# Value products of both key tiles in one step, and whole-width transposes for the gate columns, in a hybrid streaming encoder layer

## The chip, the cores and the metric

The kernel runs on one core of one Trainium2 chip. The metric is the device time of one execution in microseconds (us), lower is better. The kernel before took 2306.43 us as the median of three runs, with 2305.89 and 2309.27 at the ends. A core has a matrix engine (TensorE, "PE" in the profile; its weight loads are listed apart as "PEld"), a vector engine (VectorE, "DVE"), an engine for activation functions and copies (ScalarE, "ACT"), a general engine (GpSimd, "POOL"), a queue that issues most transfers (SyncE, "SP"), and sixteen DMA engines. TensorE reads its operands from the on-chip buffer and writes its results into banks of an accumulation memory (PSUM), from where ScalarE or VectorE copies them out.

## The reference

The kernel computes one layer of an encoder for a prompt of 2048 tokens and, beside it, eight short decode sequences of 16 tokens. Everything is float32. Cut to what matters here:

```
qm, km, vm, om, ip, fp, qa, ka, va = split_in(x @ w_in)
hm = mlstm_chunkwise(qm, km, vm, logi, logf, ...)      # 4 heads x 128, a matrix memory per head
ha = swa_prompt(rope(qa), rope(ka), va, attn_sinks)    # 8 query heads on 2 key/value heads x 64
h = layer_norm(ALPHA * x + concat(gated hm, ha) @ w_out)
y = layer_norm(ALPHA * h + conv_ffn(h))
```

The part that the change touches first is the attention over a sliding window. A query tile of 128 tokens sees its own tile and the one before, under a mask:

```
s = einsum(q, k) * 64 ** -0.5                 # per head, masked
mx = maximum(max(s), sink)
p = exp(s - mx) / (sum(exp(s - mx)) + exp(sink - mx))
o = einsum(p, v)                              # the value products
```

The second part is the matrix memory. There the weight of key s for token l is `exp(b_l - b_s + logi_s - m_l)`, with `b` the running sum of the logarithms of the forget gate and `m` a running maximum. The kernel holds these exponents as rows (one head per partition, tokens along the row) and also needs them as columns (one token per partition), since ScalarE adds a bias per partition.

## The kernel before, in words

The work has four stages on TensorE: the input projections (up to about 640 us), the output projection (to about 903 us), the up-projections of the feed-forward part (to about 1860 us) and its down-projections. The large products are done by a seven-product scheme on halves, each number split into two parts of fewer bits and multiplied in three products (lines 705, 731, 223 to 225, 1874 and 2081).

The mLSTM and the attention are woven into the first two stages. Two chains of small steps, `m_chain` (line 1044) and `a_chain` (line 1246), each a Python generator, run through the sixteen prompt tiles. A planner, `Chains` (line 158), walks over the dense products. Each dense step (six products of 256 columns, or three of 512) adds 645 to its clock. A chain's step yields its cost, which is added to the clock, the delay after which its next step is due, and how many of the five small PSUM banks the next step needs. Each request for a bank notes the time at which it is reckoned to be free: the clock plus `HOLDS`, or 3500 where the bank's name isn't in it (`bank`, line 928). A step is put into the stream as soon as the clock has passed its due time and the banks it needs are reckoned free. TensorE's order is exactly this order (`manual_schedule`, line 237); the other engines' orders are worked out by the framework from the dependences. The waits on the chip are real semaphores, so a step that the planner puts too early makes TensorE wait, and the dense products behind it wait as well.

One attention tile (`swa`, line 1272) does these steps: the scores of four heads (line 1304, tile `psc`), the exponentials and the scores of the other four, the divisions by the sums (line 1321), and then the part that the change edits. The probabilities lie with queries on partitions, in `sc`; for the value products the keys must lie on partitions. So, for each key tile, eight 128 x 128 transposes (line 1343, tile `ppt`) and two copies by ScalarE (line 1344, tile `pth`) turn them. The value products (line 1349, tile `ppo`) take the 64 columns of a head's values as the stationary operand and the 512 columns of four query heads as the moving one, one product for each half of the output's partitions. Each such product is two instructions in the profile. The step before runs the transposes of a key tile together with the value products of the key tile before:

```
for kt in range(nk + 1):
    ... transposes of key tile kt, if kt < nk ...
    ... value products of key tile kt - 1, if kt ...
```

After the first transposes the queries and keys of the next tile are turned as well (`swa_first`, line 1259, tiles `pq` and `pk`). A last copy by ScalarE (line 1356, tile `mixa`) and a store end the tile.

The mLSTM's tile (`m_tile`, line 1183) begins with `m_cols` (line 1021): the rows of exponents, four in partitions 0 to 3 and four in partitions 32 to 35 of `ay`, are turned into columns by one TensorE transpose (line 1025, tile `pcol`) and copied out by VectorE (line 1027). Then come the gate's exponentials, the scores (`pscore`), the products with the values and with the memory (`pnum`, `pcu`), the norm, and at the end four transposes of the result (line 1177, tile `pht`).

Of the kernel before, what the change touches and what calls it, by code (L numbers as in the profile page):

```python
# [14 lines left out]
P = 128  # L15
# [16 lines left out]
RING = 3  # L32

NBANKS = 5
HOLDS = {"pm": 6500, "pgr": 4000, "pnum": 5000, "ppo": 6500}

WB = 4
WR = 7
# [167 lines left out]
class Prog:  # L206
# [721 lines left out]
    def bank(self, shape, name):  # L928
        self.chains.ask(HOLDS.get(name, 3500))
        return self.tps.tile(shape, F32, name=name, tag="tb")  # L930

    def t_setup(self):
        nc, a, tp = self.nc, self.a, self.tp

        def ld(n):
            t = self.one("k_" + n, list(a[n].shape))
            nc.sync.dma_start(t, a[n])
            return t
        nc.sync.dma_start(self.ident, a["ident"])
        self.gb = ld("gb")  # L940
        self.mcau = ld("mcau")
        self.mswa = ld("mswa")
        self.seg = ld("seg")
        self.sink = ld("sink")
        self.sinkx = ld("sinkx")
        self.m0 = ld("m0")
        self.nsink = self.one("nsink", [P, 8])
        nc.vector.tensor_scalar_mul(self.nsink, self.sink, -1.0)
        nc.vector.tensor_scalar_mul(self.sink, self.sink, 8.0)
        self.gm = ld("gm")  # L950
        nc.vector.tensor_scalar_mul(self.gm, self.gm, 0.5)

        raw = self.work("kw", [36, MH])
        nc.sync.dma_start(raw, a["sel"])
        self.sel = self.one("sel", [36, MH], F32R)
        nc.vector.tensor_copy(self.sel, raw)
        self.hl = [self.one(f"hl{i}", [36, P], F32R) for i in range(2)]
        self.ay = [self.one(f"ay{i}", [36, P]) for i in range(2)]
        for i in range(2):
            nc.vector.memset(self.ay[i], 0.0)  # L960
            nc.vector.tensor_copy(self.hl[i], self.ay[i])
        self.kh, self.kl = [self.one(n, [P, RING, P], F32R) for n in ("kringh", "kringl")]
        self.kv = {}
        self.C = self.work("C", [P, MH, 129], bufs=2)
        nc.vector.memset(self.C, 0.0)

        self.M = self.row("M")
        self.mc = self.M[:, P:]
        nc.vector.memset(self.mc, 0.0)
# [51 lines left out]
    def m_cols(self, i):  # L1021

        nc = self.nc
        ps = self.bank([P, 36], "pcol")
        nc.tensor.transpose(ps, self.ay[i], self.ident[:36, :36])
        col = self.work("col", [P, 36], bufs=2)
        nc.vector.tensor_copy(col, ps)
        return col

    def m_emt(self, col):  # L1030
# [241 lines left out]
    def swa(self, t):  # L1272
        nc = self.nc
        V = nc.vector
        if self.a_first is None:
            self.swa_first(t)
            yield 550, 4000, 2
        qh, ql = self.a_first
        self.a_first = None
        r = t % RING  # L1280
        if t == 0:
            slots, nk = [0], 1
            mask = self.mswa[:, :P]
            sel = slice(0, 1)
        else:
            slots, nk = sorted([(t - 1) % RING, r]), 2
            mask = self.mswa[:, P:] if slots[1] == r else self.mswa[:, :2 * P]
            sel = slice(slots[0], slots[1] + 1, slots[1] - slots[0])
        N = nk * P
        mix = self.work("mixa", [P, 4, P])  # L1290

        def scores(j0):

            sink, nsink = [x.rearrange("p (k j) -> p k j", k=2)[:, :, j0:j0 + 2] for x in (self.sink, self.nsink)]
            sc = self.work("sc", [P, 4, 2 * P + 4], bufs=2)
            mx, sm = [self.work(n, [P, 4], bufs=2) for n in ("amx", "asm")]
            w = lambda x: x.rearrange("p (k j) -> p k j", k=2)
            nc.gpsimd.tensor_copy(sc[:, :, N:N + 1].rearrange("p (k j) o -> p k (j o)", k=2), sink)
            ps = [self.bank([P, 2, 2, P], "psc") for _ in range(2)]
            for j in range(2):  # L1300
                for i, (q, k) in enumerate(((qh, self.kh), (qh, self.kl), (ql, self.kh))):
                    for kvh in range(2):
                        rs = slice(64 * kvh, 64 * kvh + 64)
                        nc.tensor.matmul(ps[kvh][:, j, :nk], q[rs, j0 + j], k[rs, sel], start=i == 0, stop=i == 2)  # L1304
            for kvh in range(2):
                for j in range(2):
                    c = 2 * kvh + j
                    V.tensor_tensor_reduce(out=sc[:, c, :N], in0=ps[kvh][:, j, :nk].rearrange("p a b -> p (a b)"), in1=mask, scale=1.0, scalar=-3e38,
                                           op0=ALU.add, op1=ALU.max, accum_out=mx[:, c:c + 1])

            V.scalar_tensor_tensor(w(mx), w(mx), -0.125, nsink, op0=ALU.mult, op1=ALU.min)
            return sc, mx, sm

        def exps(sc, mx, sm):
            for j in range(4):
                nc.scalar.activation(sc[:, j, :N + 1], sc[:, j, :N + 1], AF.Exp, bias=mx[:, j:j + 1], scale=0.125, accum_out=sm[:, j:j + 1])

        def divided(sc, mx, sm):
            V.reciprocal(sm, sm)
            for j in range(4):  # L1320
                nc.scalar.activation(sc[:, j, :N], sc[:, j, :N], AF.Copy, scale=sm[:, j:j + 1])

        z = [scores(0)]
        yield 900, 3200, 2
        exps(*z[0])
        z.append(scores(2))
        yield 900, 3600
        exps(*z[1])
        divided(*z[0])
        if t + 1 < NPT and self.i_done > self.place(t + 1)[0]:  # L1330
            self.a_load = self.swa_dma(t + 1)
        yield 0, 3000
        divided(*z[1])
        scs = [x[0] for x in z]
        yield 0, 4200, 2 + 2 * (self.a_load is not None)

        po = pts = None
        for kt in range(nk + 1):
            new = self.work("pth", [P, 2, 512], bufs=2) if kt < nk else None
            for kvh in range(2) if kt < nk else ():  # L1340
                pp = self.bank([P, 512], "ppt")
                for j in range(4):
                    nc.tensor.transpose(pp[:, j * P:(j + 1) * P], scs[j // 2][:, 2 * kvh + j % 2, kt * P:(kt + 1) * P], self.ident)  # L1343
                nc.scalar.copy(new[:, kvh], pp)
            if kt:
                po = po or self.bank([P, 512], "ppo")
                for kvh in range(2):
                    w = self.kv[slots[kt - 1]][:, P + 64 * kvh:P + 64 * kvh + 64]
                    nc.tensor.matmul(po[64 * kvh:64 * kvh + 64], w, pts[:, kvh], start=kt == 1, stop=kt == nk)  # L1349
            pts = new  # L1350
            if kt == 0 and self.a_load is not None:

                self.swa_first(t + 1)
                self.chains.t += 550
            yield (860 if kt < nk else 0) + (1400 if kt else 0), 0 if kt == nk else 1500 if kt else 3000, 2 * (kt + 1 < nk) + (kt == 0)
        nc.scalar.copy(mix.rearrange("p a b -> p (a b)"), po)
        self.mix_out(t, 4, mix)

# [837 lines left out]
```

## Time and profile before

| what | number |
|---|---|
| median of three runs | 2306.43 us |
| profiled execution | 2306.25 us, of which the span of the trace is 2304.5 us |
| TensorE busy | 2278.9 us, 99% of the span |
| VectorE, ScalarE, GpSimd busy | 1807.4, 1272.4 and 279.4 us |
| value products, line 1349 | 124 instructions, 33.45 us of duration, from 338.9 to 858.3 us |
| columns of exponents, line 1025 | 17 instructions, from 190.5 to 825.3 us |
| moved by DMA | 632.38 MB, 274 GB/s in the mean |

A row of the timeline reads: start in us, duration in us, engine, line, operation, tile written and tiles read, form, how many instructions the row merges, and, in brackets, how long the engine was idle before and what released it. The form `128*64 128x512` is a stationary operand of 128 rows and 64 columns and a moving one of 512 columns. TensorE's instructions are pipelined, so a row's duration is longer than the distance to the next start; the starts tell the pace.

### The profile page before, as it was taken

The numbers are of one execution on the slowest core, as the hardware profiler recorded it, in microseconds if no ns is written. First come the engines' busy times: TensorE is split into PE (matmuls) and PEld (weight loads), VectorE is DVE, ScalarE is ACT, GpSimd is POOL, SyncE is SP. The second block draws the span as 40 slices with busy tenths as digits, with TensorE's granted clock in tenths as the row PEclk, the third lists the DMA queues.
The fourth block names the chain that finished last, engine by engine and source line by source line (L and its number), as shares of the span: only waits on it lengthen the run. The fifth ranks groups of instructions, "written<-read, shape, count | busy, mean of one in ns | idle before, by whom it ended". The sixth has DMA issues, their size and how long they took to land.

```text
span 2304.5 us, 39741 instructions
## 1 busy us (share of the span) xinstructions
PE 2278.9 (99%) x14293; PEld 2094.4 (91%) x14293; DVE 1807.4 (78%) x3075; ACT 1272.4 (55%) x2377; POOL 279.4 (12%) x509
## 2 busy tenths in 40 slices
PE   8999999999999999999999999999999999999998
PEld 8999999989877778999999999999999978888876
DVE  8787587787688888998778777678766786895987
ACT  5453476776766656555656555556555544444442
POOL 0001001100011210211112101003111200200200
PEclk9999999999999999999999999999999999999999
DMA  7988999899987757888777888878998786746742
GB/s 267 319 306 297 309 322 342 310 306 341 309 286 239 242 199 277 302 328 300 277 281 272 307 304 310 306 256 289 316 299 260 248 299 213 253 170 223 253 156 83
DMA packets 300165, 632.38 MB, mean 274 GB/s; under 512 B 47868, under 2 KB 141120, under 8 KB 299968
## 3 DMA queue, kind: packets, MB, share of 16 engines
q1 hardware_dynamic: 295296, 616.14, 77.3%
q0 software_dynamic: 3520, 10.56, 1.4%
q10 hardware_dynamic: 1152, 3.15, 0.4%
q8 instruction: 113, 1.85, 0.3%
q14 instruction: 84, 0.69, 0.1%
HBM read 458.11 MB, written 171.64 MB: 273 GB/s over the span
## 4 chain that ended last, share of the span: by engine, by line
PE 81%; DVE 4%; DMA 2%; issue 1%; ACT 1%; POOL 0%; SPq 0%; DVEq 0%; ACTq 0%; POOLq 0%
PE dps L1874 19%; PE fup L1874 19%; PE dps L705 8%; PE fup L2081 6%; PE dps L2081 6%; PE fht L2081 6%; PE dps L223 3%; PE dps L224 2%; PE dps L225 2%; PE ppo L1349 1%; PE psc L1304 1%; PE ppt L1343 1%; PE dps L731 1%; PE fht L1698 1%; PE pscore L1129 1%
## 5 line engine op out<-in xcount | busy, mean ns | idle before, releaser
L1874 PE MATMUL fup<-hh,uw 128*128 128x384 f32 (+1 forms) x1848 | 478.4, 328 | 0.0
L1874 PE MATMUL dps<-hh,uw 128*128 128x384 f32 (+1 forms) x1848 | 478.0, 328 | 0.0
L1874 PEld LDWEIGHTS fup<-hh,uw 128*128 128x128 f32 x1848 | 330.5, 188 | 0.0
L1874 PEld LDWEIGHTS dps<-hh,uw 128*128 128x128 f32 x1848 | 330.3, 188 | 0.0
L1932 DVE SCALAR_TENSOR_TENSOR cc<-u,cw,cc 128x768 f32<-128x768 f32 (+1 forms) x264 | 258.2, 979 | 62.8 <-ACT cc L1930 56.1
L1874 PE MATMUL fup<-hl,uw 128*128 128x384 f32 (+1 forms) x924 | 303.2, 328 | 0.9 <-DVE hl L219 0.9
L1874 PE MATMUL dps<-hl,uw 128*128 128x384 f32 (+1 forms) x924 | 302.8, 328 | 0.0
L705 PE MATMUL dps<-w,oh 128*128 128x256 f32 x1344 | 254.2, 284 | 0.0
L218 ACT CAST uw<-wraw 128x1024 fp32r<-128x1024 f32 x126 | 123.3, 979 | 230.4 <-PE dps L2081 122.4
L219 DVE TENSOR_TENSOR w<-wraw,w 128x1024 fp32r<-128x1024 f32 (+2 forms) x167 | 189.7, 1142 | 66.0 <-ACT w L218 61.9
L218 ACT CAST w<-wraw 128x1024 fp32r<-128x1024 f32 (+2 forms) x167 | 163.0, 984 | 119.0 <-PE dps L705 61.9
L705 PEld LDWEIGHTS dps<-w,oh 128*128 128x128 f32 x1344 | 210.7, 188 | 10.8 <-issue 8.1
L219 DVE TENSOR_TENSOR uw<-wraw,uw 128x1024 fp32r<-128x1024 f32 x126 | 142.5, 1131 | 62.3 <-ACT uw L218 62.2
L705 PE MATMUL dps<-w,ol 128*128 128x256 f32 x672 | 188.1, 280 | 0.0
L1874 PEld LDWEIGHTS fup<-hl,uw 128*128 128x128 f32 x924 | 173.9, 188 | 1.7 <-DVE hl L219 1.5
L2081 PE MATMUL fup<-uw,fu 128*128 128x512 f32 x726 | 174.0, 396 | 1.2 <-ACT fht L2089 1.2
L1874 PEld LDWEIGHTS dps<-hl,uw 128*128 128x128 f32 x924 | 173.8, 188 | 0.0
L705 PE MATMUL dps<-oh,w 128*128 128x256 f32 x896 | 169.6, 285 | 3.6 <-DVE w L219 1.3
L2081 PEld LDWEIGHTS fup<-uw,fu 128*128 128x128 f32 x726 | 136.6, 188 | 34.3 <-ACT fht L2089 1.6
L2081 PE MATMUL dps<-uw,fu 128*128 128x512 f32 x660 | 165.3, 396 | 1.1 <-DVE uw L219 1.1
L1930 ACT ACTIVATE cc<-u,cw 128x768 f32<-128x768 f32 (+1 forms) x132 | 132.0, 1001 | 46.2 <-DVE u L1912 22.2
L2081 PEld LDWEIGHTS dps<-uw,fu 128*128 128x128 f32 x660 | 124.1, 188 | 31.2 <-DVE uw L219 1.5
(318 smaller groups left out, 4590.0 us busy)
## 6 DMA issues: line engine op xcount, KB each, us to landing
uw<-zw SPq DMA_DIRECT2D x176, 512.0 KB, 5.1
zw<-uw SPq DMA_DIRECT2D x88, 512.0 KB, 3.3
w<-zws SPq DMA_DIRECT2D x72, 512.0 KB, 5.8
wv<-wup SPq DMA_DIRECT2D x66, 512.0 KB, 4.4
wraw<-wi SPq DMA_DIRECT2D x65, 512.0 KB, 5.5
wraw<-zt SPq DMA_DIRECT2D x60, 512.0 KB, 4.1
wraw<-wdn SPq DMA_DIRECT2D x45, 512.0 KB, 4.5
wraw<-wo SPq DMA_DIRECT2D x40, 512.0 KB, 4.7
```

What stands on the lines that cost most here:

```text
L218: nc.scalar.copy(hi, src)
L219: return nc.vector.tensor_sub(lo, src, hi.bitcast(F32)).ins
L223: mm(out, ah, bh, start=start, stop=False)
L224: mm(out, ah, bl, start=False, stop=False)
L225: mm(out, al, bh, start=False, stop=stop)
L705: mm(o, l, r, start=s in (1, 7) and c == k == i == 0, stop=k == 3 and i == 2, skip_group_check=True)
L731: mm(o, x, w, start=k == i == 0, stop=k == KD - 1 and i == 2, skip_group_check=True)
L1129: self.nc.tensor.matmul(ps[:, h], qk[:, 4 + h], qk[:, h], start=True, stop=True)
L1874: mm(ps, l[:, k], r[:, k], start=s in (1, 7) and k == 0 and i == 0, stop=k == 3 and i == 2, skip_group_check=True)
L1930: S.activation(c[:, v], u[:, 2:2 + n], AF.Identity, bias=w[3], scale=w[2])
L1932: V.scalar_tensor_tensor(c[:, v], u[:, i:i + n], w[i], c[:, v], op0=ALU.mult, op1=ALU.add)
L2081: mm(ps, l[:, k, c], r[:, k], start=s in (1, 4, 7) and u == 0 and k == 0 and i == 0, stop=u == nu - 1 and k == n - 1 and i == 2, skip_grou ...
```

## The change

In `swa`, the transposes and copies of both key tiles now come first, each in a step of its own, with both turned tiles kept. The value products of both key tiles follow as one step. For two key tiles the costs that the planner is told add up as before (860 + 860 + 2800 in place of 860 + 2260 + 1400). The delays are 1500 and then 3000 in place of 3000 and then 1500. The output bank is asked for only at the products, and its reckoned hold goes from 6500 to 5000.

In `m_cols`, the rows `ay` now span 128 partitions, cleared once at the start, and are turned with the whole 128 x 128 identity in place of its first 36 rows and columns. Only the first 36 columns of the result are copied out, as before.

```diff
-HOLDS = {"pm": 6500, "pgr": 4000, "pnum": 5000, "ppo": 6500}
+HOLDS = {"pm": 6500, "pgr": 4000, "pnum": 5000, "ppo": 5000}
...
-        self.ay = [self.one(f"ay{i}", [36, P]) for i in range(2)]
+        self.ay = [self.one(f"ay{i}", [P, P]) for i in range(2)]
         for i in range(2):
             nc.vector.memset(self.ay[i], 0.0)
-            nc.vector.tensor_copy(self.hl[i], self.ay[i])
+            nc.vector.tensor_copy(self.hl[i], self.ay[i][:36])
...
-        ps = self.bank([P, 36], "pcol")
-        nc.tensor.transpose(ps, self.ay[i], self.ident[:36, :36])
+        ps = self.bank([P, P], "pcol")
+        nc.tensor.transpose(ps, self.ay[i], self.ident)
         col = self.work("col", [P, 36], bufs=2)
-        nc.vector.tensor_copy(col, ps)
+        nc.vector.tensor_copy(col, ps[:, :36])
...
-        po = pts = None
-        for kt in range(nk + 1):
-            new = self.work("pth", [P, 2, 512], bufs=2) if kt < nk else None
-            for kvh in range(2) if kt < nk else ():
+        pts = []
+        for kt in range(nk):
+            new = self.work("pth", [P, 2, 512], bufs=2)
+            for kvh in range(2):
                 pp = self.bank([P, 512], "ppt")
                 for j in range(4):
                     nc.tensor.transpose(pp[:, j * P:(j + 1) * P], scs[j // 2][:, 2 * kvh + j % 2, kt * P:(kt + 1) * P], self.ident)
                 nc.scalar.copy(new[:, kvh], pp)
-            if kt:
-                po = po or self.bank([P, 512], "ppo")
-                for kvh in range(2):
-                    w = self.kv[slots[kt - 1]][:, P + 64 * kvh:P + 64 * kvh + 64]
-                    nc.tensor.matmul(po[64 * kvh:64 * kvh + 64], w, pts[:, kvh], start=kt == 1, stop=kt == nk)
-            pts = new
+            pts.append(new)
             if kt == 0 and self.a_load is not None:
 
                 self.swa_first(t + 1)
                 self.chains.t += 550
-            yield (860 if kt < nk else 0) + (1400 if kt else 0), 0 if kt == nk else 1500 if kt else 3000, 2 * (kt + 1 < nk) + (kt == 0)
+            yield 860, 3000 if kt + 1 == nk else 1500, 1 if kt + 1 == nk else 2
+        po = self.bank([P, 512], "ppo")
+        for kt in range(nk):
+            for kvh in range(2):
+                w = self.kv[slots[kt]][:, P + 64 * kvh:P + 64 * kvh + 64]
+                nc.tensor.matmul(po[64 * kvh:64 * kvh + 64], w, pts[kt][:, kvh], start=kt == 0, stop=kt + 1 == nk)
+        yield 1400 * nk, 0
```

## The prediction

> **What bounds the kernel now.** I read the page first (busy shares, the chain that ended last), then the stretches in which the two chains of small steps run, then what TensorE waited for there, then TensorE's timeline row by row around the two edited places.
>
> ```profile
> span 2304.5 us, 39741 instructions
> ...
> PE 2278.9 (99%) x14293; PEld 2094.4 (91%) x14293; DVE 1807.4 (78%) x3075; ACT 1272.4 (55%) x2377; POOL 279.4 (12%) x509
> ...
> PE 81%; DVE 4%; DMA 2%; issue 1%; ACT 1%; POOL 0%; SPq 0%; DVEq 0%; ACTq 0%; POOLq 0%
> ```
>
> ```profile
> 300.00:640.00 340.00, 335.83 (x2787) 309.78 (x2786) 258.59 (x749) 242.98 (x625) 32.63 (x56) 1.00 0.94 322
> 640.00:860.00 220.00, 219.86 (x1237) 171.01 (x1236) 184.24 (x470) 140.45 (x359) 38.39 (x46) 1.00 0.71 241
> ```
>
> ```profile
> PE pnum L1212 <- issue: 1.9, 2, 1.4
> ...
> PE ppo L1349 <- ACT pth L1344: 0.6, 1, 0.6
> ```
>
> TensorE is busy 99% of the span and holds 81% of the chain. Both edits act between 300 and 860 us, where the small steps are woven into the projections (columns of the stretches: length, busy time of PE, PEld, DVE, ACT, POOL, granted clock, DMA share, GB/s). PE idles 4.2 us of 340 in the first stretch and 0.1 of 220 in the second, at a granted clock of 1.00. The last two rows are from its waits between 300 and 860 (in total, times, longest). So a microsecond taken from TensorE's own stream is a microsecond of the run, unless something else falls due. The nearest candidate is the DMA share of 0.94 before 640.
>
> **The value products.** The rows of one key tile, TensorE's timeline (start, duration of the row, line, count), and one row of the chain between them:
>
> ```profile
> 395.98 1.03 PE L1343 MATMUL ppt<-ident,sc 128*128 128x128 f32 x8
> 396.85 0.60 PE L1241 MATMUL pq<-ident,qa 128*128 128x128 f32 x4
> 397.29 0.27 PE L1243 MATMUL pk<-ident,kva 128*128 128x128 f32 x1
> ...
> 401.26 0.60 PE L1343 MATMUL ppt<-ident,sc 128*128 128x128 f32 x4
> 401.79 0.65 PE L1349 MATMUL ppo<-pth,kva 128*64 128x512 f32 x2
> 402.27 0.60 PE L1349 MATMUL ppo<-pth,kva 128*64 128x512 f32 x2
> 402.80 0.38 PE L705 MATMUL dps<-w,oh 128*128 128x256 f32 x1
> 403.02 0.28 PE L705 MATMUL dps<-w,ol 128*128 128x256 f32 x1
> ...
> 405.34 0.28 PE L705 MATMUL dps<-w,oh 128*128 128x256 f32 x1
> 405.55 0.25 PE L1025 MATMUL pcol<-ident,ay 36*128 36x36 f32 x1
> 405.73 1.08 PE L1349 MATMUL ppo<-pth,kva 128*64 128x512 f32 x4
> ```
>
> ```profile
> 397.56 3.43 PE dps L705 x30
> ```
>
> The paces first. Four transposes take 396.85 to 397.29, 0.11 us each; the 30 dense products go at 3.43 / 30, 0.115 each. A value product is two instructions, and the two heads' halves start together (one row of x2): call such a row a pass. The second pass starts 0.48 after the first (402.27 against 401.79).
>
> Now the price of entering and leaving the 64-column form. The four transposes from 401.26 have streamed by 401.26 + 4 x 0.11 = 401.70; the second dense product starts at 403.02, that is 1.32 later. Two passes at 0.48 and one dense product make 1.07. So 0.25 us per visit is neither pass nor product: 0.09 ahead of the first pass, the rest around the first dense product (402.80 to 403.02 is 0.22 instead of 0.115).
>
> Today each of the query tiles 1 to 15 visits that form twice, after the transposes of key tile 1 and again later; tile 0 visits it once, before and after the change alike. The change makes it one visit with four passes, so it removes 15 visits, while the passes and transposes stay. What the trace does not show is the pace from the second to the third pass, whose weights are new. Bounds: 0.43 (the first pass ends at 401.79 + 0.65 = 402.44, the second at 402.27 + 0.60 = 402.87) and 0.53 (the second pass to the next dense product, 402.27 to 402.80). At 0.48, the nearest row because it is pass to pass, a merge saves 0.25; at the ends, with the inner pace at 0.43 too, 0.35, or 0.20. 15 x 0.25 = 3.8 us; ends 3.0 and 5.2. The Trainium skill, TensorEngine Tiling (Array Packing), section Key Properties, says that only a change of tiling mode drains TensorE, not a change of tile; by that the third pass pays nothing new and the sum is the one taken, whereas with the upper pace it would be 0.8 less.
>
> **The columns of the exponents.** They are a 36-row transpose today. Two more places:
>
> ```profile
> 337.57 0.28 PE L705 MATMUL dps<-oh,w 128*128 128x256 f32 x1
> 337.78 0.25 PE L1025 MATMUL pcol<-ident,ay 36*128 36x36 f32 x1
> ...
> 338.18 0.28 PE L705 MATMUL dps<-ol,w 128*128 128x256 f32 x1
> ...
> 338.65 0.28 PE L705 MATMUL dps<-oh,w 128*128 128x256 f32 x1
> 338.86 0.65 PE L1349 MATMUL ppo<-pth,kva 128*64 128x512 f32 x2
> ...
> 372.08 0.25 PE L1025 MATMUL pcol<-ident,ay 36*128 36x36 f32 x1
> ...
> 825.32 0.25 PE L1025 MATMUL pcol<-ident,ay 36*128 36x36 f32 x1
> ```
>
> ```profile
> L1025 PE MATMUL pcol<-ident,ay x17: 216/249/253, 190.5 to 825.3; 36*128 36x36 f32 x17
> ```
>
> There are 17 (last row). Alone between dense products, one costs 337.57 to 338.18, 0.61, less two dense products (0.23): 0.38. With 128 rows and 128 columns it becomes an ordinary transpose at 0.11, so 0.27 goes; three stand alone (304, 337, 757 us): 0.8. In 13 tiles it stands directly ahead of the second visit (the first at 372.08, the last at 825.32). There it adds 405.34 to 405.73, 0.39, less the 0.21 that the visit's entry takes without it (338.65 to 338.86): 0.18, of which 0.07 goes: 0.9. The seventeenth stands behind other 36-row products and counts as nothing. Together 1.7 us. The lower end is below nothing and is rival 2. The wider tile, its clearing once at the start, and the 36 columns copied out of 128 cost the vector engine nothing new: the copy keeps its shape.
>
> **What moves.** The order is written out by the planner's sums (one dense step is six products, 645 of its units), so it can be worked by hand from the code. Today five steps lie between the two groups of transposes (the x30 row) and three between the second visit and the transposes before it, less the products. After the change the second transposes are due after 1500, but need two free banks, which the reckoned hold of 3500 gives after four steps; the products follow after five more. Costs charged per tile stay 9070 (2200 of one chain, 6870 of the other), and following a whole round gives 31 dense steps per tile as now, so the chains end at the same place in the dense work and the last output block gets its tiles no later. No DMA is moved: the loads of the next tile are issued ahead of this step, the store of the result behind it. The output bank is asked for later and the hold shortened to 5000, which matches; its predecessor in the ring of five is by then a bank copied out long ago.
>
> New is that all four copies by ScalarE must be ready in one piece, and behind a waiting product stands all dense work of TensorE. From the first transposes to the products it is 1.33 (395.98 to 397.31) + 24 x 0.115 + 8 x 0.11 + 0.1 + 30 x 0.115, plus 0.5 for the small transposes between and 0.2 for the entry: 9.2 us. Today's first transposes of three tiles, and the second pair of ScalarE's copies in each:
>
> ```profile
> 362.45 1.04 PE L1343 MATMUL ppt<-ident,sc 128*128 128x128 f32 x8
> ...
> 541.72 1.04 PE L1343 MATMUL ppt<-ident,sc 128*128 128x128 f32 x8
> ...
> 548.36 1.08 PE L1349 MATMUL ppo<-pth,kva 128*64 128x512 f32 x4 [0.64 <-ACT pth L1344]
> ...
> 609.58 1.03 PE L1343 MATMUL ppt<-ident,sc 128*128 128x128 f32 x8
> ```
>
> ```profile
> 368.00 1.07 ACT L1344 COPY pth<-ppt 128x512 f32<-128x512 f32 x2 [1.00 <-PE ppt L1343]
> ...
> 549.32 1.07 ACT L218 CAST w<-wraw 128x1024 fp32r<-128x1024 f32 x1
> 550.26 1.09 ACT L1344 COPY pth<-ppt 128x512 f32<-128x512 f32 x2
> ...
> 618.10 1.08 ACT L1344 COPY pth<-ppt 128x512 f32<-128x512 f32 x2
> ```
>
> In the tiles at 541 and 609 the last copy ends 9.6 us after the first transposes (551.35 and 619.18), the latest of the fifteen (one more at 507 is like them); there products would wait up to 0.4, together 1.2 us. Against that the wait of 0.64 at 548.36, for the first key tile's copies, goes. If ScalarE's copies move forward with their transposes, the 1.2 goes too. Net between -0.6 and +0.6; I take nothing.
>
> **The sum.** -3.8 - 1.7 = -5.5 us. The profiled execution took 2306.25 (span 2304.5 and 1.75 around it), 0.18 below the median of the three runs, 2306.43. So 2306.25 - 5.5 = 2300.75, on the median's scale 2300.9, 0.24% less. The forecast's own ends: -(5.2 + 1.7) - 0.6 gives 2298.9; -(3.0 + 1.7) + 0.6 gives 2302.3.
>
> **The rivals.**
> 1. The loads take the gain back before 640. Eight of the fifteen tiles lie there: 8 x (0.25 + 0.07) and two lone columns (0.54), 3.1 us. The 0.94 speaks for it; against it, no row of TensorE's waits there names a DMA, and the worst (1.4 at pnum) comes once. Then only 2.4 remains: 2304.0, within 0.2%.
> 2. The time around the 36-row transpose is not due to its form and stays, and 92 more columns are streamed: 17 x 0.11 x 92/128 = +1.3 us in place of -1.7, total -2.5: 2303.9. Against it: the entry to the 64-column form shows the same 0.21 with quite other operands. The Trainium skill, TensorEngine Tiling (Array Packing), section Instruction Overhead, speaks for it: a matmul has some 60 cycles of overhead, so that 36 columns cost no less than 60, and 128 cost more.
> 3. Slower: ScalarE's order puts the second pair of copies behind three more casts of the weights (1.07 each, 3.2) in the eight tiles before 640. Their last copies end 6.6 us after the first transposes in the first of the eight (369.07 against 362.45) and 9.6 in the last (609), 8.3 in the mean of all; 3.2 later makes 11.5, so products wait 2.3 in each: 8 x 2.3 = 18.4, less 5.5, +12.9: 2319.2. It decides from 4.6 + 5.5 = 10.1 us in all on, 1.3 per tile, two casts. For it: at 548.36 the first pair of copies was ready only 6.6 us after its transposes began. Against it: five of the eight tiles have over a microsecond in hand, and ScalarE is busy 71% there.
>
> **How the numbers follow.** Forecast 0.62, rival 1 0.14, rival 2 0.13, rival 3 0.11. What a measurement of this kernel tells from no change is about 0.2%, 4.6 us, so faster means below 2301.8. Of the forecast's share 0.04 falls above that. Faster 0.58; same 0.04 + 0.14 + 0.13 = 0.31; slower 0.11. The range takes in the forecast and rivals 1 and 2 with half a microsecond of spread at either end, 2298.2 to 2304.8, and leaves out rival 3 and the forecast's tails.
>
> **What would show it.** Right: rows of eight value products in place of two of four, the gap of 0.09 and the doubled first dense product once per tile; the column rows as 128*128 with 0.11 to the next start; no 0.64 wait at ppo; 24 dense products between the two groups of transposes. The forecast is wrong if the wait of ppo for pth exceeds 1 us in all, if TensorE's waits between 300 and 640 name loads, or if the third pass starts more than 0.53 after the second.

## The result and the profile after

The changed kernel is slower, by little: 2310.74 us as the median of 22 runs (2307.14 to 2314.66) against 2306.75 for the kernel before in its own 22 runs (2303.51 to 2313.78). The ratio is 1.0016, with a 95% interval of 1.001 to 1.0023. The forecast was 2300.9, in a range up to 2304.8. The profiled execution, 2314.66 us, is the slowest of the 22; what it shows beyond the median has to be told apart from what every execution pays.

The page of the changed kernel, the lines that answer to those of before (span, busy times, shares of the chain):

```profile
span 2312.9 us, 39733 instructions
...
PE 2278.3 (99%) x14293; PEld 2097.4 (91%) x14293; DVE 1807.8 (78%) x3075; ACT 1269.2 (55%) x2377; POOL 270.2 (12%) x509
...
PE 27%; DVE 2%; DMA 1%; ACT 0%; issue 0%; SPq 0%; DVEq 0%; POOL 0%; ACTq 0%; POOLq 0%
```

The chain is followed back only to a transfer at 1617 us here, so it says nothing about the two woven stages. The stretches do (same columns as before; changed kernel):

```profile
300.00:640.00 340.00, 331.49 (x2764) 308.49 (x2763) 254.75 (x735) 237.01 (x606) 31.04 (x56) 0.99 0.93 320
640.00:860.00 220.00, 215.56 (x1223) 171.31 (x1222) 186.85 (x480) 141.32 (x369) 34.29 (x45) 0.99 0.72 239
```

TensorE now idles 4.4 us of 220 after 640, where it idled 0.1, and 8.5 instead of 4.2 before it. Its waits in the changed kernel (in total, times, longest) name the places:

```profile
PE ppt L1343 <- ACT sc L1321: 4.3, 2, 4.0
PE dps L705 <- ACT dps L800: 3.1, 1, 3.1
PE ppt L1519 <- POOL v L1094: 2.8, 1, 2.8
```

The third was there before (2.9). The first two are new, and neither was forecast: the first transposes of a tile wait for the divided scores near 820 us, and a dense product waits near 530 us for ScalarE to copy out a bank of the projections. No wait of `ppo` for `pth` is listed, and none for a load.

**The edits themselves worked.** TensorE's timeline around one merged visit of the changed kernel, and the second of the two visits of the kernel before:

```profile
405.65 0.28 PE L705 MATMUL dps<-w,oh 128*128 128x256 f32 x1
405.86 1.94 PE L1355 MATMUL ppo<-pth,kva 128*64 128x512 f32 x8
407.73 0.38 PE L705 MATMUL dps<-w,oh 128*128 128x256 f32 x1
407.95 0.28 PE L705 MATMUL dps<-w,ol 128*128 128x256 f32 x1
```

```profile
405.34 0.28 PE L705 MATMUL dps<-w,oh 128*128 128x256 f32 x1
405.55 0.25 PE L1025 MATMUL pcol<-ident,ay 36*128 36x36 f32 x1
405.73 1.08 PE L1349 MATMUL ppo<-pth,kva 128*64 128x512 f32 x4
406.74 0.38 PE L705 MATMUL dps<-w,oh 128*128 128x256 f32 x1
406.96 0.28 PE L705 MATMUL dps<-w,ol 128*128 128x256 f32 x1
```

After: from 405.65 to 407.95 is 2.30, less two dense products (0.23) 2.07. Before: the second visit is 405.34 to 406.96, 1.62, less two dense products and the 0.18 of the columns 1.21; the first visit, from the prediction's rows, is 401.70 to 403.02 less one dense product, 1.21. So two visits of 2.42 became one of 2.07: 0.35 saved per tile, where 0.25 was reckoned. The four passes take (1.94 - 0.59) / 3 = 0.45 from start to start. The columns in the changed kernel:

```profile
404.13 0.28 PE L705 MATMUL dps<-w,oh 128*128 128x256 f32 x1
404.25 0.27 PE L1025 MATMUL pcol<-ident,ay 128*128 128x128 f32 x1
...
404.48 0.28 PE L705 MATMUL dps<-w,ol 128*128 128x256 f32 x1
```

From 404.13 to 404.48 less two dense products is 0.12, where the 36-row form standing alone cost 0.38. The merged visit takes the same in all fifteen tiles (1.86 or 1.87 us from its first product to the next instruction). In the 13 tiles in which the columns stood ahead of the second visit 0.18 became 0.12; with the three that stood alone that is some 1.5 us. The rows thus show some 15 x 0.35 + 1.5 = 7 us less work on TensorE, and yet the run is 4 us longer in the median, and 8.4 in the profiled execution. Some 11 and 15 us had to come from elsewhere.

**Where they came from.** The two new waits in TensorE's timeline, and the granted clock in stretches around them (length, busy time of PE, granted clock, DMA share, GB/s):

```profile
529.73 0.28 PE L705 MATMUL dps<-oh,w 128*128 128x256 f32 x1
533.06 0.58 PE L705 MATMUL dps<-w,oh 128*128 128x256 f32 x1 [3.06 <-ACT dps L800]
...
818.11 0.38 PE L1343 MATMUL ppt<-ident,sc 128*128 128x128 f32 x2
822.47 1.73 PE L1343 MATMUL ppt<-ident,sc 128*128 128x128 f32 x6 [3.98 <-ACT sc L1321]
```

```profile
526.00:529.50 3.50, 3.50 (x34) 1.00 1.09 378
529.50:533.00 3.50, 0.50 (x5) 0.87 1.02 336
533.00:536.00 3.00, 2.94 (x14) 0.50 1.01 406
536.00:539.00 3.00, 3.00 (x16) 0.52 1.05 409
539.00:542.00 3.00, 3.00 (x28) 1.00 1.01 403
...
822.40:825.60 3.20, 3.13 (x13) 0.50 0.83 284
```

Each wait is followed by a stretch at half clock, 5.8 us of work behind the first (533.06 to 538.9) and 3.1 behind the second. Work at half clock takes twice as long, so the waits cost 2.9 and 1.6 us more than their own length. Together 3.1 + 2.9 + 4.0 + 1.6 = 11.6 of the 15 us in this execution; the rest lies in shorter waits and was not divided further.

The wait at 818 can be followed back. VectorE and ScalarE of the changed kernel, in their own order:

```profile
814.31 1.28 DVE L1573 SCALAR_TENSOR_TENSOR ymix<-ymix,lsc,o_ln_b 128x1024 f32<-128x1024 f32 x1
...
817.30 1.22 DVE L898 TENSOR_TENSOR ol<-xraw,oh 128x1024 fp32r<-128x1024 f32 x1
818.44 0.16 DVE L1160 TENSOR_TENSOR mr<-mr,bmv 128x4 f32<-128x4 f32 x1
818.51 1.28 DVE L1614 SCALAR_TENSOR_TENSOR ymix<-ymix,dps 128x512 f32<-128x512 f32 x2
819.71 0.17 DVE L1319 RECIPROCAL asm<-asm 128x4 f32<-128x4 f32 x1
```

```profile
819.79 1.28 ACT L1167 ACTIVATE hn<-hn,ms 128x128 f32<-128x128 f32 x4 [2.37 <-POOL ms L1161]
820.98 1.03 ACT L218 CAST w<-wraw 128x1024 fp32r<-128x1024 f32 x1
821.91 1.70 ACT L1321 ACTIVATE sc<-sc,asm 128x256 f32<-128x256 f32 x4
```

At the end of an output block VectorE has a burst of large operations (1.2 to 1.3 us each). Two operations of 0.16 us stand between them: the one that ends the scale of the normalised heads (818.44, after which GpSimd and then ScalarE go on) and the reciprocal (819.71) that the divided scores need. ScalarE, in order, then does the heads, a cast, and the scores at 821.91, and TensorE's transposes wait until 822.47.

Why they meet here and not before is seen in TensorE's order. The rows around the numerators of the same tile, kernel before, then changed kernel:

```profile
798.89 0.39 PE L1304 MATMUL psc<-kringh,qh 64*128 64x256 f32 x2
...
801.97 1.05 PE L1129 MATMUL pscore<-qk 128*128 128x128 f32 x8
...
809.94 1.06 PE L1221 MATMUL pcu<-v,kw 128*128 128x129 f32 x8
815.71 1.04 PE L1343 MATMUL ppt<-ident,sc 128*128 128x128 f32 x8
```

```profile
799.10 1.05 PE L1129 MATMUL pscore<-qk 128*128 128x128 f32 x8
...
802.62 0.38 PE L1304 MATMUL psc<-kringh,qh 64*128 64x256 f32 x2
...
808.86 1.06 PE L1221 MATMUL pcu<-v,kw 128*128 128x129 f32 x8
818.11 0.38 PE L1343 MATMUL ppt<-ident,sc 128*128 128x128 f32 x2
```

The second scores of a tile (`psc`) stood ahead of the mLSTM's scores and now stand behind them. The first transposes stood 21 dense products of 512 columns behind the numerators and the memory's update (`pcu`); now it is 36. In the planner's steps of three, the attention chain has slipped five steps against the mLSTM chain. That holds for all seven tiles whose first transposes lie in the output stage, from 653 us on; in the input stage the order is the one that the prediction worked out, with 24 dense products between the two groups of transposes.

The slip begins between the stages. The last products of the input stage (line 731, the gates and keys, 48 instructions in eight dense steps) run under `hold` (line 632): the planner's clock goes on and no step of a chain is put in. Around this pause, kernel before, then changed kernel:

```profile
619.33 1.08 PE L1349 MATMUL ppo<-pth,kva 128*64 128x512 f32 x4
...
626.98 0.27 PE L1008 MATMUL pgr<-ident,g 128*4 128x128 f32 x1
```

```profile
629.61 0.27 PE L1008 MATMUL pgr<-ident,g 128*4 128x128 f32 x1
...
629.92 1.94 PE L1355 MATMUL ppo<-pth,kva 128*64 128x512 f32 x8
```

Before, the tile's value products stand ahead of the pause. In the changed kernel they are due some steps later, fall behind it, and the next tile's first scores follow a dense step later; from there on the mLSTM's scores stand between the two groups of `psc`. Worked through without this one hold, the planner of the changed kernel keeps its order of the input stage to the end, with eight dense steps from `pcu` to the first transposes (nine in the last tile).

### The profile page after: what moved, and what is told of

Same layout as the page of the kernel before. It is cut to its first block, busy times and chain, and to the rows that moved or that the text cites. A ratio compares the mean times of both kernels' runs of the same rounds, so it can differ in the third digit from the quotient of the medians.

```text
span 2312.9 us, 39733 instructions
## 1 busy us (share of the span) xinstructions
PE 2278.3 (99%) x14293; PEld 2097.4 (91%) x14293; DVE 1807.8 (78%) x3075; ACT 1269.2 (55%) x2377; POOL 270.2 (12%) x509
```

## The experiments

The first theories. A: the two edits are worth what TensorE's rows show, and the loss comes from the moved order. B: it comes from merging the products themselves. C: any edit reorders the queues of the other engines (the framework works their order out anew), and that decides. All twelve kernels were compared with the kernel before, run beside them on the same chip.

**The columns alone**, in the kernel before:

```diff
-        ps = self.bank([P, 36], "pcol")
-        nc.tensor.transpose(ps, self.ay[i], self.ident[:36, :36])
+        ps = self.bank([P, P], "pcol")
+        nc.tensor.transpose(ps, self.ay[i], self.ident)
```

> The columns part alone on the kernel before: the rows of exponents span 128 partitions and are turned with the whole identity; TensorE's order is that of the kernel before. Theory A (the mode prices are real and the loss of the changed kernel comes from its moved order): 1.7 us less than before, perhaps 2.3. Theory B (the loss belongs to the merged products themselves): the same here. Theory C (any edit reshuffles the other engines' orders, and the time scatters by some microseconds for that alone): between -4 and +4, with new waits of TensorE on ScalarE in the trace.

Measured: 2306.97 us, ratio 0.9996 (0.9987 to 1.0004). A gain of the size forecast for this part (1.7 us, 0.07%) lies within the interval, and so does none. By the starts of its rows the part saves 1.5 us on TensorE.

**The merged products without the columns**: the changed kernel with the 36-row transpose put back.

> The changed kernel with the columns turned as before (36 rows): the value products alone, in the moved order. Theory A: the changed kernel's time plus 1.7 to 2.3 us, some 6 us over the kernel before, with the two long waits of TensorE on ScalarE still there. Theory B: the same. Theory C: anywhere from -4 to +8.

Measured: 2317.64 us, ratio 1.0044 (1.0032 to 1.0056). The wait for the divided scores is 7.4 us in three places, the longest 5.2. One of the two waits that A named is there, but the size is a miss: 0.28% over the changed kernel by the ratios, 6.5 us, where the columns alone were to cost 1.7 to 2.3.

**The changed kernel's order, the products in two visits again**, one dense step apart:

```diff
-            yield 860, 3000 if kt + 1 == nk else 1500, 1 if kt + 1 == nk else 2
+            yield 860, (2355 if nk == 2 else 3000) if kt + 1 == nk else 1500, 1 if kt + 1 == nk else 2
...
-        yield 1400 * nk, 0
+            yield 1400, 0
```

> The changed kernel's order, but the value products of the first key tile are issued one dense step ahead of those of the second, as two visits to the 64-column form. Theory A: the waits of the changed kernel stay and the merge's gain goes, 15 x 0.36 to 0.42 = 5.4 to 6.3 us slower than the changed kernel. Theory B: not slower than the changed kernel, since no four copies have to be ready in one piece. Theory C: within 4 us of either.

Measured: 2316.53 us, ratio 1.0035 (1.0021 to 1.0049), with a wait of 3.6 us for the divided scores at 821 us. Not merging does not bring the time back; by the ratios it is 0.19%, 4.4 us, longer than the changed kernel, near the 15 x 0.35 that merging is worth. B falls.

**Both edits in the old order**: the products of both key tiles at the place of the old second visit, the planner's costs, delays and holds as before.

```diff
+            if kt == nk:
+                for k in range(nk):
+                    for kvh in range(2):
+                        w = self.kv[slots[k]][:, P + 64 * kvh:P + 64 * kvh + 64]
+                        nc.tensor.matmul(po[64 * kvh:64 * kvh + 64], w, pts[k][:, kvh], start=k == 0, stop=k + 1 == nk)
+            pts.append(new)
```

> Both parts, but the merged value products stand where the second visit stood, with the planner's figures of the kernel before, so that TensorE's order is that of the kernel before except that the first visit's products have moved to the second. Theory A: the whole gain of the modes without the moved order's waits, 6 to 7 us less than before, and the wait of 0.64 us of products for the first pair of copies gone. Theory B: not faster than before. Theory C: between -10 and -2, with waits at other places.

Measured: 2304.24 us, ratio 0.9989 (0.998 to 0.9999), faster than the kernel before, if by little (the interval ends just under 1), and 0.27% under the changed one. So the same two edits gain where the order stays. The gain is some 2.5 us, not the 6 to 7 that A expected. In the profiled execution TensorE idles 7.1 us between 300 and 640 where it idled 4.2 before, with longer waits for the numerators near 498 us (2.1 us) and behind the copies of `pth` near 548 us (1.8 us); that is 2.9 us of the difference.

**Is it the slip?** Two kernels with one delay changed. In the first the changed kernel's second delay goes from 3000 to 1700, so that the transposes stand 21 dense products behind `pcu` again; in the second the kernel in the old order gets 2150 for 1500, so that its chain slips.

> The changed kernel with one planner figure changed: the delay behind the second transposes is 1700 instead of 3000, so that the attention chain doesn't slip behind the recurrent chain in the output stage (its first transposes stand 7 dense steps behind the numerators again, as in the kernel before, not 12). Theory A (the loss of the changed kernel is the place of the attention chain against the recurrent chain): the 4 us wait of the first transposes for the divided scores near 818 us goes, and with it the half clock behind it; 2300 to 2305 us. Rival D (any order other than the old one meets waits of its own, wherever the chain stands): waits of 15 to 23 us over the woven stretch as in the other reordered kernels, 2308 to 2315 us.

> The kernel with the products in place of the second visit and both parts in it, with one planner figure changed (the delay ahead of the products 2150 instead of 1500), so that the attention chain slips behind the recurrent chain as in the changed kernel (first transposes 12 dense steps behind the numerators in the output stage). Theory A: 2309 to 2315 us, with a wait of 3 us or more of the first transposes for the divided scores in the output stage. Rival D, and the rival that the loss lies in the place of the merged products alone: within 2 us of the kernel in place, 2302 to 2307 us.

Measured: 2317.69 us, ratio 1.005 (1.0037 to 1.0063), and 2325.21 us, ratio 1.0077 (1.0065 to 1.0089). The second is slower than even A had it. Its waits for the divided scores are 9.9 us in six places, none as long as the 3 us named (the longest 2.7), and it isn't the clean test that was meant: its chain slips already at an earlier pause, from 470 us on, so that two of the six waits lie in the input stage. The first was a miss for A. It has no wait for the divided scores, but others, at the end of the output stage among them (waits and stretch of this kernel):

```profile
PE fht L1699 <- DMA hst<-zh: 6.2, 2, 4.1
```

```profile
640.00:860.00 220.00, 219.15 (x1252) 174.19 (x1251) 191.60 (x494) 142.66 (x367) 34.83 (x46) 1.00 0.75 252
860.00:930.00 70.00, 63.37 (x304) 51.63 (x303) 47.98 (x58) 37.23 (x57) 4.94 (x5) 0.93 0.62 222
```

It loses almost nothing from 640 to 860, as A says of a chain that hasn't slipped, and then 6.6 us of the next 70 to waits, 6.2 of them for a load, and more to the half clock behind them. Before 640 it idles 10.0 us, where the kernel before idles 4.2. Why that load comes late in this order was not followed up, and the profiled execution is the slowest of six (2324.8 us). Rival D, that any order but the old one meets waits of its own, named the sign of this run; the time is beyond its range too (2308 to 2315).

**Is the load at 519 us the root of the wait at 530?** In the changed kernel VectorE waits 3.27 us at 519.5 for a pair of rows of `wdn`, and ScalarE's exponentials and copies come late behind it. Two kernels, the changed one and the one in the old order, load these pairs by turns into two sets of buffers, one pair ahead:

```diff
-            self.txy = x, y = [self.xp.tile([P, D], F32, name="txy", tag=f"xr{q}", bufs=1) for q in (1, 3)]
+        self.txy[k] = x, y = [self.xp.tile([P, D], F32, name="txy", tag=f"xr{q}", bufs=1) for q in ((1, 3) if k % 2 == 0 else (2, 4))]
...
+            if ahead and k + 1 < NK2:
+                self.sums_load(k + 1)
```

> The changed kernel, its order on TensorE unchanged, with the loads of the pairs of wdn rows that VectorE subtracts near 480 to 557 us put into two sets of buffers by turns and issued one pair ahead. If VectorE's wait of 3.3 us for that load at 519.5 us is the root of TensorE's wait of 3.1 us at 530 us: that wait and the half clock behind it (3.4 us) go, and the time is 5 to 7 us below the changed kernel's, some 2304 to 2306 us. Rival (ScalarE's and VectorE's queues are full there anyway, or the waits move): within 2 us of the changed kernel, 2309 to 2313 us.

> The kernel with the products in place and both parts, with the same loads issued one pair ahead. If that load is the root of TensorE's waits at 498 us (2.1 us for the numerators) and 548 us (1.8 us at the transposed heads): both go, 2300 to 2302 us. Rival (the waits move): 2303 to 2306 us. It would be the fastest of all if the first holds.

Measured: 2312.55 us, ratio 1.0022 (1.0013 to 1.0031), and 2305.01 us, ratio 0.999 (0.9981 to 0.9998). Neither differs from the kernel it was made from. In the first the long wait at 530 us is gone (0.7 us in all for line 800), which fits the late load as its root, but the median is no lower. Either that wait is rare in the changed kernel, whose profiled execution is the slowest of 22, or the new order of the queues loses as much elsewhere; the runs don't tell which. The wait for the scores is still there, 4.0 us:

```profile
PE ppt L1349 <- ACT sc L1327: 4.3, 2, 4.0
```

**The cross.** Both structures in one kernel, by tile: the changed kernel's for the tiles below 8 and the old order's from 8 on ("mix_i"), and the reverse ("mix_o"). TensorE's order is then the changed kernel's in one stage and the old order's in the other. The tile at the pause, tile 8, goes with the output stage, and with it the place of its value products before or behind the pause.

```diff
+        if t < 8:
             pts = []
...
+        else:
+            po, pts = None, []
```

> The changed kernel's step structure for the attention tiles of the input stage (tiles below 8) and the structure with the products in place of the second visit for those of the output stage: TensorE's order is the changed kernel's in the first and that of the kernel in place in the second, tile for tile. Theory O (the changed kernel loses in the output stage, where its attention chain stands 5 dense steps late: the wait of 4 us for the divided scores, the half clock behind it and the pairs of transposes that run into their bank): 2303 to 2306 us and no such wait. Theory I (it loses in the input stage, by the 3 us wait near 530 us and the half clock behind it): 2309 to 2313 us.

> The opposite cross: products in place of the second visit in the input stage (tiles below 8), the changed kernel's structure and order in the output stage. Theory O: 2308 to 2312 us, with a wait of 3 us or more of the first transposes for the divided scores near 815 us. Theory I: 2302 to 2306 us.

Measured: 2306.59 and 2315.19 us (the second would give 1.0037 by the medians alone). The ratios, each to the kernel before run beside it, with the two kernels at the other corners:

| order in the input stage | output stage: old order | output stage: the changed kernel's |
|---|---|---|
| old | 0.9989 (0.998 to 0.9999) | 1.0026 (1.0016 to 1.0037) |
| the changed kernel's | 0.9995 (0.9984 to 1.0005) | 1.0016 (1.001 to 1.0023) |

The output stage decides: its order makes 0.29% in the mean of the two rows ((1.0026 + 1.0016 - 0.9989 - 0.9995) / 2), 6.7 us. The order of the input stage makes nothing that can be told from zero. The stretch from 640 to 860 shows it, in "mix_i" and then in "mix_o":

```profile
640.00:860.00 220.00, 219.87 (x1243) 173.55 (x1242) 185.86 (x470) 139.69 (x356) 40.73 (x46) 1.00 0.71 240
```

```profile
640.00:860.00 220.00, 213.33 (x1192) 167.97 (x1191) 181.95 (x468) 139.03 (x363) 35.97 (x45) 0.98 0.71 235
```

The idle time of TensorE there is 0.1 us in both kernels whose output stage has the old order, 4.4 in the changed kernel and 6.7 in "mix_o", whose wait for the divided scores is 3.9. For the changed kernel, 4.3 more and 1.6 for the half clock behind the wait make 5.9 of the 6.7. All fourteen profiles divide in the same way. In the seven kernels whose first transposes stand 36 products behind `pcu`, TensorE idles 4.4 to 9.2 us from 640 to 860; in the seven with 21 it is 0.1 in five, 0.9 in the one with the delay of 1700, and 2.8 in one that follows.

**The queue as the root.** The four small operations put ahead in VectorE's queue, in the changed kernel and in the one in the old order; TensorE's order stays:

```diff
+        with self.tc.high_priority():
+            V.scalar_tensor_tensor(r, emt, 1e18, r, op0=ALU.min, op1=ALU.max)
+            V.scalar_tensor_tensor(r, r, EPS, r, op0=ALU.mult, op1=ALU.mult)
+            V.tensor_add(r, r, mv[:, :, 1])
...
+            with self.tc.high_priority():
+                V.reciprocal(sm, sm)
```

> The changed kernel with TensorE's order unchanged and four small VectorE operations put ahead in its queue: the three of 128x4 that end in the scale of the normalised heads, and the reciprocal of the sums of the scores. In the changed kernel they stand behind five operations of 1.2 us near 815 to 820 us, and ScalarE waits for them ahead of the divided scores. If that queue is the root of TensorE's 4 us wait: the wait shrinks to under 1 us, and the time is 3 to 6 us below the changed kernel's, 2305 to 2308 us. Rival (ScalarE's casts are the bound there, or the new order on VectorE waits elsewhere): within 2 us of the changed kernel or slower, 2309 to 2315 us.

> The kernel in place with the same four small operations put ahead. It has no wait for divided scores, so there is nothing to win by them: 2303 to 2306 us if a new order on VectorE and ScalarE costs nothing by itself; 2307 to 2312 us if any new order of these queues meets waits of its own (rival D).

Measured: 2310.91 us, ratio 1.0018 (1.0009 to 1.0027), and 2311.28 us, ratio 1.0018 (1.0008 to 1.0027). In the changed kernel the wait for the scores is gone from the list, so VectorE's queue was its root. But dense products now wait for a split operand from VectorE, and TensorE idles 5.2 us from 640 to 860, no less than the 4.4 in the changed kernel:

```profile
PE dps L225 <- DVE ol L898: 3.9, 2, 2.6
PE dps L705 <- ACT dps L800: 3.3, 2, 2.0
```

The second kernel is the plainest test of C: the same edits and the same order on TensorE as the kernel in the old order, only VectorE, ScalarE and the load queue ordered anew around four small operations, and 0.29% slower. C is right that such an order alone can cost this much. It isn't right that any edit does: "mix_i" has TensorE's whole input stage reordered and pays nothing that can be measured against the kernel in the old order.

What the twelve runs leave: the changed kernel loses about 6.7 us to the place of its attention chain in the output stage. There small VectorE operations of the chain fall behind the block's burst of large ones. That is shown as the root of the longest wait, but not as the whole price, since the wait can be taken away and the time stays. Nor has a run brought the chain back to its place in the changed kernel and won the time. Without the slip the two edits are worth 0.1%, as the kernel in the old order shows (0.9989, and 0.999 with the loads ahead). Of the 7 us that TensorE's rows show some 2.5 are left; 2.9 went into the waits before 640 us in the profiled execution, and what took the rest is open.

## Why the prediction was wrong, step by step

- **The value products** were right in kind and too small: 0.35 per tile and 5.2 us in all, not 0.25 and 3.8. The mis-sized term is the pace inside the visit, 0.45, near its lower bound of 0.43, not 0.48. The Trainium skill, TensorEngine Tiling (Array Packing), section Key Properties (only a change of mode drains), agrees: the third pass, with new weights and no change of mode, pays nothing beyond that pace of 0.45.
- **The columns** came out as reckoned, 0.12 in place of 0.38 when alone, about 1.5 of 1.7 us by the rows. Rival 2 falls by the rows; the times of the columns alone can't tell.
- **"What moves" is the step that failed.** It said that following a whole round gives 31 dense steps per tile as now, "so the chains end at the same place", and that the order therefore costs nothing. The period is the same. But two chains with the same period can stand differently to one another, and I followed one round of the input stage, without the pause between the stages. Behind that pause the same delays leave the attention chain five steps further back against the mLSTM chain. That a dense step of the output stage has three products instead of six is not the reason: the planner counts 645 for either, a tile takes 33.3 us in both stages (the first transposes from 395.98 to 429.27, and from 782.40 to 815.71), and the kernel with the delay of 2150 slips to the same place, twelve dense steps, within the input stage. The step looked at one wait, that of `ppo` for `pth`, and there it was right (none is listed). It did not ask which other engine's small operations the moved steps would now stand behind. They stand behind VectorE's burst at the end of a block. TensorE idles 4.3 us more from 640 to 860 and loses 1.6 in clock, and by the cross this stage's order costs 6.7 us, as much as the two edits save.
- **Rival 1** (loads take the gain back) is not what happened: no load is among TensorE's new waits, and the DMA share before 640 is 0.93. At second hand one load counts, that of `wdn` at 519 us behind the wait at 530; with it ahead the median was no lower. **Rival 3** had the right sign and the right idea, ScalarE late and TensorE behind it, at the wrong place and for another reason: the divided scores of the output stage, held up by VectorE, not the copies of `pth` before 640.
- **The signs named as proof** were met: rows of eight, 0.12 for the columns, no wait at `ppo`, in the input stage 24 dense products between the transposes (12 of twice the width in the output stage, four steps in both). None of the signs of being wrong was seen. All of them concern the edited places and the waits that were thought of, and a kernel can meet them all and be slower.

## What to carry to other kernels

Where several chains of small steps are woven into one stream by a planner, an edit of a step's delay can be an edit of the phase between the chains, above all where the weaving pauses and a step falls behind the pause that stood ahead of it; write the order down on both sides of every pause, before and after, and look at what the moved steps now stand behind on the other engines. An edit that saves time on the bound engine is first tried without moving anything else: here that version gained and the re-planned one lost. Where other engines' queues are ordered by a framework, a gain of 0.3% on TensorE is as large as what a reordering of those queues around four small operations cost here, so several orders are worth measuring.

## What the runs showed of the hardware

A wait of TensorE can cost more than its length. In the first two stages, each of the seven waits of 3.06 us or more, in six kernels, was followed by some 3.4 or 6.8 us at a granted clock of 0.50; the wait of 2.8 to 2.9 us for `v` near 250 us, which all fourteen profiles have, in one of them. Shorter waits are not safe either: of the twelve of 2.04 to 2.71 us between 300 and 910 us, in all profiles, seven were followed by such a stretch (one of 2.09 us in the kernel with the four operations ahead in the old order) and five not (one of 2.39 us in the kernel with the delay of 1700). The Trainium skill, TensorE: Matmul & The Clock Gate, section Why this matters for your kernels, asks for no gaps above some 3 us. The seven longest waits agree; the shorter ones show that a gap below it can cost the clock too. The same clock is behind part of the scatter between executions of one kernel. In the profiles of the kernel before and of "mix_i" a stretch near the start of the run reads:

```profile
10.50:16.50 6.00, 5.55 (x24) 0.50 1.03 421
```

```profile
10.50:16.50 6.00, 5.27 (x29) 1.00 1.03 420
```

With half clock in that stretch and one near 42 us, about 10 us in all, an execution is by estimate some 5 us longer than one without (10 us at half clock do the work of 5), as much as the whole difference studied here. Two of the fourteen profiles have none of it, those of "mix_i" (2300.46 us) and of the columns alone (2300.72 us), and each is the fastest of its twelve. A profile of one execution shows where time can go, and only the medians show what a kernel loses as a rule.
